# One-hot rows of the gate tables as products on VectorE, and the key lookup a tile at a time

## The chip, the cores and the metric

The kernel runs on one core of one Trainium2 chip. The metric is the device time of one execution in microseconds, as the median of several runs. Before the change it is 2661.93 us, the median of three runs (2655.82 to 2664.12).

## The reference, cut to what matters

One step of a decoder layer is computed for 512 prompt tokens and 8 x 4 sample tokens: retention, sparse attention with an indexer, two layer norms, and a layer of 128 x 128 = 16384 single-neuron experts. Only the experts' part touches the change:

```python
v1, i1 = lax.top_k(s1, PEER_TOPK)      # 16 best keys of 128, first half of the query
v2, i2 = lax.top_k(s2, PEER_TOPK)      # the same for the second half
cand = (v1[..., :, None] + v2[..., None, :]).reshape(T, PEER_HEADS, 256)
cidx = (i1[..., :, None] * PEER_NKEYS + i2[..., None, :]).reshape(T, PEER_HEADS, 256)
sc, sel = lax.top_k(cand, PEER_TOPK)   # 16 best sums of a head
eidx = jnp.take_along_axis(cidx, sel, axis=-1)
g = jax.nn.softmax(sc, axis=-1)
act = gelu(einsum('td,thkd->thk', xb, u[eidx]))
out = einsum('thk,thkd->td', g * act, v[eidx])
```

Each token has 8 heads, and each head chooses 16 experts, so a token has 128 triples of a first key, a second key and a gate.

## The kernel before, in words

The tokens stand in five tiles: four of 128 prompt tokens, and one with the sample group's 32 tokens four times over, on whose rows two heads stand where a prompt tile has eight. Matrix products in float32 are made of three products of two parts each (`mm3`); a weight's parts come from ScalarE (L126, the high part) and a subtract (L127, the low part, on VectorE or, for every other early product, on GpSimd).

Up to some 1320 us come the projections, the attention, the first layer norm and the scores of the keys. Then three stages follow.

*The choosing* (`choose`, L1187). For each tile VectorE finds the 16 best sums of each head, works out the place of each in the two lists, and looks up both keys. The lookup (L1243 to L1255) goes half by half and four heads at a time: GpSimd subtracts the numbers 0 to 15 (`iota`) from each place, so that a zero marks the place (L1247, `oh`, 128x1024); VectorE turns each head's zeros into the key there and everything else into 0 (L1251, 128x256, four of them); and VectorE adds each row of 16 (L1254). The tiles 0 and 4 come first, beside the embedding branch on TensorE; their experts are later fetched row by row. Then the three dense tiles 1, 2 and 3.

*The gate tables* (`gate_tables`, L1259). For a dense tile the chosen keys and gates are transposed by TensorE, so that the 128 choices stand on partitions and the tokens along the rows (`pkT`). For each token there are two one-hot matrices [128 choices, 128 keys]: `o1` for the first key, `o2` for the second, times the gate. Their product on TensorE (L1282) is the token's gates over all 128 x 128 experts. It goes eight tokens at a time: GpSimd subtracts the second key from the iota (L1273), VectorE compares the first key with the iota (L1275) and turns GpSimd's zeros into gates (L1277); all three are 128x1024. Four tokens' products fill a bank, ScalarE copies it out (L1283), and after 32 tokens a 2 MB store to DRAM follows. There are 3 tiles x 4 quarters of 32 tokens x 4 steps of eight, 48 steps. `o1` and `o2` have three buffers each.

*The experts* (from L1411). For 128 pieces of 128 experts TensorE makes the products with U (24 matmuls of 384 columns), gelu and gate follow, then the products with V (18 matmuls of 512 columns).

Two kinds of work fill waits: early products with U (`u_early`, L938), whose result goes to SBUF (22 of them at most, only while the tables are made) or to DRAM and back; and gathered rows (`gather_tile`, L1287): GpSimd issues an indirect DMA for one expert of each of 128 tokens (L1303), and VectorE uses it (L1316 for U, L1322 for V). A planner decides how many: each step of a stage yields the microseconds it claims of TensorE, VectorE and ScalarE, and `tick` (L953) adds them up and issues an early product (3.9 of TensorE) whenever the sum of TensorE is behind, and a row (1.15 of VectorE) for each 3.4 us of TensorE's sum. In `choose` the claims are `cost` = 0.85 (0.34 for the tile with two heads) times 0.8, four times 1.6, 3.0, 2.0 and, for the lookup, four times 2.3; the 48 steps of the tables claim 1.8, 2.3 and 1.2 each. Products that are not made early remain for the experts' stage.

Every engine works in the order of the code; loads are issued on SP's queue, stores on ScalarE's.

Of the kernel before, what the change touches and what calls it, by code (L numbers as in the profile page):

```python
# [11 lines left out]
F32 = mybir.dt.float32  # L12
F32R = mybir.dt.float32r
BF = mybir.dt.bfloat16
I32 = mybir.dt.int32
U32 = mybir.dt.uint32
AF = mybir.ActivationFunctionType
OP = mybir.AluOpType
AX = mybir.AxisListType
# [6 lines left out]
EPS = 1e-5  # L26
# [6 lines left out]
TOPK = 256  # L33
# [45 lines left out]
def tile_hybrid_step(ctx: ExitStack, tc: tile.TileContext, io):  # L79
# [24 lines left out]
    def moments(pieces, p0, p1, name):  # L104
        """1/sqrt(var + EPS) and -mean/sqrt(var + EPS) of the rows of [p, <= 512] views; the root by Newton's steps."""
# [23 lines left out]
    # ---------------------------------------------------------------- pools of the front  # L129
# [19 lines left out]
    def weights(src, n=1024, eng=V, raw=None, keep=None):  # L149
        """A [128, n] piece of a weight as its two float32r parts."""  # L150
        raw = raw or wst.tile([128, 1024], F32, name="wraw")
        load(raw[:, :n], src)
        h, l = keep or (wst.tile([128, 1024], F32R, name="wh"), wst.tile([128, 1024], F32R, name="wl"))
        split(h[:, :n], l[:, :n], raw[:, :n], eng)
        return h, l
# [21 lines left out]
    def project(chunk, evac):  # L177
        """Columns of a 128-wide chunk of W_in, transposed: [128, tokens]."""
# [8 lines left out]
    def project_nat(pieces, width, hook=lambda u: None, part=None):  # L187
        """Columns of W_in as they come: five tiles [128 tokens, columns]; pieces: (source, number of k), for width
        columns after the other. part: a tile for the sample group's four sums, each in 32 columns of the array (four
        k a piece); the fifth tile is then that group's alone."""  # L190
# [31 lines left out]
    def gates(n, tile_of):  # L222
        """Gates of the branches: the next chunks, as tanh(x / 2), to DRAM."""
# [6 lines left out]
    # ---------------------------------------------------------------- attention keys, indexer  # L230
# [29 lines left out]
    # places of the pages  # L260
# [17 lines left out]
    for i, t0 in enumerate(TILES):  # L278
# [3 lines left out]
        # keys of the attention, rotated  # L282
# [12 lines left out]
        # indexer keys: layer norm, rotated  # L295
# [43 lines left out]
    def rope_swap(dst, raw, cs, sn, blk, u, eng):  # L339
        """Rotation of rows in a chunk whose heads are blocks of 2*blk rows; sn has the source rows' signs."""  # L340
# [11 lines left out]
    # ---------------------------------------------------------------- queries of the attention  # L352
# [20 lines left out]
    # ---------------------------------------------------------------- indexer of the prompt  # L373
# [37 lines left out]
    # ---------------------------------------------------------------- indexer of the sample group  # L411
    # rows 32 q + 4 b + t: the q-th quarter of the past of token t of sequence b, then (q = 3) the new keys
# [64 lines left out]
    # the TOPK-th largest of each row, bit by bit; y = +-x so that it is not negative  # L477
# [6 lines left out]
    def row_sum(which):  # L484
        """Sum of cnt[:, which] over the four quarters of a row, on each of them."""
# [4 lines left out]
    def bisect_start():  # L490
        V.tensor_scalar(junk, scq, 0.0, None, op0=OP.is_ge, op1=OP.add, accum_out=cnt[:, 0:1])
        p = row_sum(0)
        # sign, and how many of y reach the value looked for
# [15 lines left out]
    def bisect_end():  # L509
# [3 lines left out]
        # how many of the equal ones are taken: the first of them  # L513
# [19 lines left out]
    # ---------------------------------------------------------------- retention  # L533
# [20 lines left out]
    def rotated(h, out):  # L554
        """q and k of a head, rotated; steps."""
# [15 lines left out]
    def group_norm(on, h, p, rows, sg, dst):  # L571
        """Rows of one head, normed over its 512 columns, turned, scaled and gated: dst [128, 4, rows]."""
# [11 lines left out]
    def head(h, prev, qk, ahead):  # L584
# [4 lines left out]
        # q, k  # L589
# [7 lines left out]
        # v  # L597
# [17 lines left out]
        # decayed k as it comes, for the states  # L615
# [9 lines left out]
        # sample: k four times over; parts of k and of the scores on rows 0:64 (high) and 64:128 (low)  # L625
# [20 lines left out]
        # gate  # L646
# [13 lines left out]
        def state_after():  # L660
            """State after the prompt."""
# [10 lines left out]
        # prompt: o[i] = sum over j <= i, two tiles of queries at a time  # L672
# [32 lines left out]
    def sample(h, kcs, srs, vst, qm, sgs):  # L705
        """Retention of the sample group, two sequences at a time."""
# [54 lines left out]
    # ---------------------------------------------------------------- queries, gates, attention of the prompt  # L761
    ASC = float(np.float32(128 ** -0.5))
    def softmax(x, src):
        """exp(ASC * (src - max)) / sum into x, over the rows of src."""
# [8 lines left out]
    def prompt_attention(aw):  # L773
        """The pieces of the attention of the prompt."""
# [32 lines left out]
    def sample_attention(st):  # L807
        """The pieces of the attention of the sample group, to be run one after another."""
# [18 lines left out]
        for g in range(2):  # L827
# [3 lines left out]
            for part in range(9):  # L831
# [13 lines left out]
            # of this part alone: its maximum, the sum of its exponentials, their product with V;  # L845
                # a part with no chosen key has zeros
# [22 lines left out]
            # the parts together  # L869
# [45 lines left out]
    # ---------------------------------------------------------------- rest of the layer up to PEER  # L915
# [5 lines left out]
    def layer_norm(x, rows, gb, eng=G):  # L921
        """In place, on a [rows, 1024] view."""
# [5 lines left out]
    # Work that fills the waits of the others: products with U whose V follows later, rows of the gathered experts.  # L928
# [24 lines left out]
    def tick(pe, dve, act=0.0):  # L953
        """After work of so many microseconds of the engines: as much of the filling as keeps them even."""
# [17 lines left out]
    def branch(rp, hook, done):  # L972
        """The sum of both branches, gated: its parts, [128, 8, tokens]. hook: other work, between the pieces; done:
        what has to come before the second branch, returns the pool of the result."""
# [46 lines left out]
    def project_out(hp, b4, brh, brl, brs):  # L1021
        """W_out and the residual: hs, [128 tokens, 1024] for each tile; steps for the tiles of FIRST."""
# [642 lines left out]
```

## Time and profile before

| | us |
|---|---|
| median of three runs | 2661.93 |
| profiled execution, span | 2726.3 |
| TensorE busy | 2478.5 |
| VectorE busy | 1934.1 |
| GpSimd busy | 993.5 |
| ScalarE busy | 953.4 |

The profiled execution gives its span, from the first to the last instruction; a time around it is not given. PE is TensorE, PEld its weight load, DVE VectorE, ACT ScalarE, POOL GpSimd, SP the queue of loads. A line of the table by stretches has the stretch and its length, then the busy time and the number of instructions of PE, PEld, DVE, ACT and POOL, the granted TensorE clock (1 is full), the DMA engines' busy share and GB/s. A line of the groups has source line, engine, operation, output and inputs, shapes and count, then the busy time in us and the mean ns of one, and at last the engine's idle time before them and what ended it. A line of the timeline has the start, the length, engine, line and operation; a bracket gives the idle time before it. An instruction's length includes the time that it was held up after its start.

### The profile page before, as it was taken

The page shows a single profiled execution, that of the slowest core. Times are in us where ns is not written, and L with a number is a line of the kernel's source. Part 1 is how long each engine was busy: PE and PEld are TensorE (multiplying, and loading weights), DVE is VectorE, ACT ScalarE, POOL GpSimd, SP SyncE. Part 2 cuts the span into 40 slices and gives each one's busy share as a digit, 9 for nine tenths or more (in the row PEclk, how much of TensorE's full clock was granted, in tenths as well). Part 3 has the DMA queues.
Part 4 walks back from the last instruction along what each step waited for, and adds up shares of the span by engine and source line. Part 5 has one row for each costly group of instructions (what it writes and reads, how often), then busy time and mean ns, then how long its engine had stood idle before and what let it go on. Part 6 is the DMA issues. An engine that isn't in the chain of part 4 may idle for free.

```text
span 2726.3 us, 40425 instructions
## 1 busy us (share of the span) xinstructions
PE 2478.5 (91%) x15162; PEld 2164.6 (79%) x15162; DVE 1934.1 (71%) x3867; ACT 953.4 (35%) x1657; POOL 993.5 (36%) x773
## 2 busy tenths in 40 slices
PE   8789999999988999999887777789999999999996
PEld 8768988888655569889777766778988988888885
DVE  6685667755322245578999999977777877877777
ACT  3232333333232333243222354543333333333332
POOL 4530000001134412110356778833444444443442
PEclk9889999999998999999998998899999999999998
DMA  6322243545675554232256566579888888998883
GB/s 204 106 85 92 71 167 113 195 127 191 226 227 156 152 173 160 96 138 72 93 184 203 201 224 223 206 259 349 294 317 310 315 321 306 332 319 308 300 314 126
DMA packets 233013, 562.71 MB, mean 206 GB/s; under 512 B 26576, under 2 KB 96400, under 8 KB 230896
## 3 DMA queue, kind: packets, MB, share of 16 engines
q1 hardware_dynamic: 140576, 287.83, 31.2%
q0 software_dynamic: 58368, 205.55, 21.6%
q10 hardware_dynamic: 33872, 66.73, 6.6%
q8 instruction: 119, 1.95, 0.3%
q14 instruction: 78, 0.64, 0.1%
HBM read 491.08 MB, written 68.95 MB: 205 GB/s over the span
## 4 chain that ended last, share of the span: by engine, by line
PE 65%; DVE 19%; issue 5%; DMA 4%; another core or an unknown queue 2%; ACT 2%; POOL 1%; SPq 0%; ACTq 0%; DVEq 0%; POOLq 0%
PE ps L160 7%; PE ps L158 7%; PE ps L159 7%; PE po L159 6%; PE po L158 6%; PE po L160 6%; PE act L158 4%; PE act L159 4%; PE act L160 4%; DVE o L1277 2%; DVE junk L1316 2%; PE nat L158 2%; PE nat L160 2%; DVE acc L1322 2%
## 5 line engine op out<-in xcount | busy, mean ns | idle before, releaser
L126 ACT ACTIVATE wh<-wraw 128x1024 fp32r<-128x1024 f32 (+2 forms) x265 | 278.7, 1052 | 606.3 <-PE ps L159 207.8
L127 DVE TENSOR_TENSOR wl<-wraw,wh 128x1024 fp32r<-128x1024 f32 (+2 forms) x239 | 306.0, 1280 | 172.7 <-ACT wh L126 150.1
L1303 POOL DMA_INDIRECT rows<-u_rows,eidx x160 | 240.3, 1502 | 317.8 <-DVE junk L1316 254.4
L1303 POOL DMA_INDIRECT rows<-v_rows,eidx x160 | 240.9, 1505 | 278.9 <-DVE acc L1322 192.5
L159 PE MATMUL po<-vl,ah 128*128 128x512 f32 x768 | 301.5, 393 | 6.6 <-DVE vl L127 6.6
L158 PE MATMUL po<-vh,ah 128*128 128x512 f32 x768 | 299.7, 392 | 1.1 <-ACT vh L126 1.1
L160 PE MATMUL po<-vh,al 128*128 128x512 f32 x768 | 300.1, 391 | 0.0
L158 PE MATMUL ps<-xh,wh 128*128 128x272 f32 x960 | 284.6, 296 | 9.3 <-issue 7.7
L159 PE MATMUL ps<-xl,wh 128*128 128x272 f32 x960 | 281.8, 294 | 8.1 <-issue 8.1
L160 PE MATMUL ps<-xh,wl 128*128 128x272 f32 x960 | 283.1, 295 | 5.9 <-issue 5.9
L160 PE MATMUL ps<-x1h,wl 128*128 128x384 f32 (+1 forms) x616 | 205.2, 333 | 28.4 <-DVE wl L127 16.8
L1322 DVE SCALAR_TENSOR_TENSOR acc<-rows,co,acc 128x1024 f32<-128x1024 f32 x160 | 227.1, 1420 | 4.4 <-DMA rows<-v_rows,eidx 3.8
L158 PE MATMUL act<-x1h,wh 128*128 128x384 f32 x664 | 225.2, 339 | 1.3 <-ACT gl L1456 1.3
L159 PE MATMUL act<-x1l,wh 128*128 128x384 f32 x664 | 223.3, 336 | 0.0
L160 PE MATMUL act<-x1h,wl 128*128 128x384 f32 x664 | 223.2, 336 | 0.0
L1316 DVE SCALAR_TENSOR_TENSOR junk<-rows,x1n 128x1024 bf16<-128x1024 f32 x160 | 212.7, 1329 | 5.8 <-DMA rows<-u_rows,eidx 5.3
L158 PE MATMUL ps<-x1h,wh 128*128 128x384 f32 (+1 forms) x616 | 206.4, 335 | 11.0 <-ACT pph L1179 8.0
L159 PE MATMUL ps<-x1l,wh 128*128 128x384 f32 (+1 forms) x616 | 202.7, 329 | 0.3 <-DVE x1l L1081 0.3
L158 PEld LDWEIGHTS ps<-xh,wh 128*128 128x128 f32 x960 | 185.6, 193 | 21.2 <-issue 13.9
L821 POOL DMA_INDIRECT kv<-ckv,idp x128 | 123.3, 963 | 211.2 <-PE nat L862 153.7
L159 PEld LDWEIGHTS ps<-xl,wh 128*128 128x128 f32 x960 | 185.8, 194 | 11.4 <-issue 10.6
L160 PEld LDWEIGHTS ps<-xh,wl 128*128 128x128 f32 x960 | 185.4, 193 | 8.1 <-issue 7.5
(448 smaller groups left out, 6121.5 us busy)
## 6 DMA issues: line engine op xcount, KB each, us to landing
wraw<-u_t SPq DMA_DIRECT2D x128, 512.0 KB
vr<-v_rows SPq DMA_DIRECT2D x128, 512.0 KB
wraw<-w_t SPq DMA_DIRECT2D x60, 512.0 KB
gg<-gd SPq DMA_DIRECT2D x33, 768.0 KB
gd<-stg ACTq DMA_DIRECT2D x12, 2048.0 KB
state<-state_ret SPq DMA_DIRECT2D x32, 512.0 KB
ret_sample<-state ACTq DMA_DIRECT2D x32, 512.0 KB
wraw<-w_rv SPq DMA_DIRECT2D x16, 512.0 KB
```

The source lines that it names most:

```text
L126: S.activation(h, x, AF.Copy)
L127: eng.tensor_tensor(l, x, r32(h), op=OP.subtract)
L158: T.matmul(out, lh, rh, start=first, stop=False)
L159: T.matmul(out, lh, rl, start=False, stop=False)
L160: T.matmul(out, ll, rh, start=False, stop=last)
L821: G.indirect_dma_start(out=kv[-1][:, i, :], out_offset=None, in_=io["ckv"], in_offset=bass.IndirectOffsetOnAxis(ap=idp[:, c:c + 1], axis=0))
L1277: V.scalar_tensor_tensor(o2, o2, 0.0, pkT[:, 2, tok, None].to_broadcast([128, 8, 128]), op0=OP.is_equal, op1=OP.mult)
L1303: G.indirect_dma_start(out=r, out_offset=None, in_=io[kind + "_rows"], in_offset=bass.IndirectOffsetOnAxis(ap=idx[:, p:p + 1], axis=0))
L1316: i = V.scalar_tensor_tensor(junk, r, 1.0, x, op0=OP.mult, op1=OP.mult, accum_out=dots[:, p % 16:p % 16 + 1])
L1322: i = V.scalar_tensor_tensor(acc, r, co[:, p % 16:p % 16 + 1], acc, op0=OP.mult, op1=OP.add)
```

## The change

Two places change. In the lookup both GpSimd's subtract and the division into groups of four heads go: for a whole tile and half, VectorE compares the places with the iota, multiplies by the keys, and adds the rows; the claims of these steps become 2.2 and 4.4 per half. In the tables each key is written as 8 a + b. For 32 tokens at a time VectorE makes one-hot rows of 16 for a and of 8 for b (with the gate in the second key's row of 8), and the one-hot row of 128 is their product, eight tokens an instruction. GpSimd has no part in either. The rest of the diff takes comments and docstrings out of the file.

```diff
@@ choose
-            for hh in range(0, nh, 4):
-                g = min(nh, 4)
-                oh = pw.tile([128, 16 * g, 16], F32, name="oh", tag="oh")
-                G.tensor_tensor(oh, abf[:, half, 16 * hh:16 * (hh + g), None].to_broadcast([128, 16 * g, 16]),
-                                iota[:, None, 0:16].to_broadcast([128, 16 * g, 16]), op=OP.subtract)
-                o4 = oh.rearrange("p (h k) a -> p h k a", h=g)
-                for h in range(g):
-                    V.scalar_tensor_tensor(o4[:, h], o4[:, h], 0.0,
-                                           ixf[:, hh + h, half, None, :].to_broadcast([128, 16, 16]),
-                                           op0=OP.is_equal, op1=OP.mult)
-                V.tensor_reduce(i12[:, half, 16 * hh:16 * (hh + g)], oh, AX.X, OP.add)
-                yield 0.0, cost * 2.3, 0.0
+            oh = pw.tile([128, n, 16], F32, name="oh", tag="oh")
+            V.tensor_tensor(oh, abf[:, half, :, None].to_broadcast([128, n, 16]),
+                            iota[:, None, 0:16].to_broadcast([128, n, 16]), op=OP.is_equal)
+            yield 0.0, cost * 2.2, 0.0
+            o4 = oh.rearrange("p (h k) a -> p h k a", h=nh)
+            V.tensor_tensor(o4, o4, ixf[:, :, half, None, :].to_broadcast([128, nh, 16, 16]), op=OP.mult)
+            V.tensor_reduce(i12[:, half, :], oh, AX.X, OP.add)
+            yield 0.0, cost * 4.4, 0.0
@@ gate_tables
+            up = gb.tile([128, 2, 128], I32, name="up", bufs=1)
+            lo = gb.tile([128, 2, 128], F32, name="lo", bufs=1)
+            upf = gb.tile([128, 2, 128], F32, name="upf", bufs=1)
+            V.tensor_copy(up, pkT[:, 0:2])
+            V.tensor_scalar(up, up, 3, None, op0=OP.logical_shift_right)
+            V.tensor_copy(upf, up)
+            V.scalar_tensor_tensor(lo, upf, -8.0, pkT[:, 0:2], op0=OP.mult, op1=OP.add)
             for q in range(4):
                 stg = gb.tile([128, 128, 32], F32, name="stg", bufs=2)
+                hot16 = gb.tile([128, 2, 32, 16], F32, name="hot16", bufs=1)
+                hot8 = gb.tile([128, 2, 32, 8], F32, name="hot8", bufs=1)
+                tq = slice(32 * q, 32 * q + 32)
+                for half in range(2):
+                    V.tensor_tensor(hot16[:, half], upf[:, half, tq, None].to_broadcast([128, 32, 16]),
+                                    iota[:, None, 0:16].to_broadcast([128, 32, 16]), op=OP.is_equal)
+                    V.tensor_tensor(hot8[:, half], lo[:, half, tq, None].to_broadcast([128, 32, 8]),
+                                    iota[:, None, 0:8].to_broadcast([128, 32, 8]), op=OP.is_equal)
+                V.tensor_tensor(hot8[:, 1], hot8[:, 1], pkT[:, 2, tq, None].to_broadcast([128, 32, 8]), op=OP.mult)
                 for c in range(0, 32, 8):
-                    tok = slice(32 * q + c, 32 * q + c + 8)
+                    ct = slice(c, c + 8)
                     o1 = gb.tile([128, 8, 128], F32, name="o1", bufs=3)
                     o2 = gb.tile([128, 8, 128], F32, name="o2", bufs=3)
-                    G.tensor_tensor(o2, iota[:, None, :].to_broadcast([128, 8, 128]),
-                                    pkT[:, 1, tok, None].to_broadcast([128, 8, 128]), op=OP.subtract)
-                    V.tensor_tensor(o1, iota[:, None, :].to_broadcast([128, 8, 128]),
-                                    pkT[:, 0, tok, None].to_broadcast([128, 8, 128]), op=OP.is_equal)
-                    V.scalar_tensor_tensor(o2, o2, 0.0, pkT[:, 2, tok, None].to_broadcast([128, 8, 128]),
-                                           op0=OP.is_equal, op1=OP.mult)
+                    for half, o in enumerate((o1, o2)):
+                        V.tensor_tensor(o.rearrange("p t (a b) -> p t a b", b=8),
+                                        hot16[:, half, ct, :, None].to_broadcast([128, 8, 16, 8]),
+                                        hot8[:, half, ct, None, :].to_broadcast([128, 8, 16, 8]), op=OP.mult)
```

## Rows read from the trace of the kernel before

**Rows 1.** The page's busy line: engine, us, share of the span, instructions.
```profile
PE 2478.5 (91%) x15162; PEld 2164.6 (79%) x15162; DVE 1934.1 (71%) x3867; ACT 953.4 (35%) x1657; POOL 993.5 (36%) x773
```
**Rows 2.** Busy time by stretches: the choosing, the tables, the experts.
```profile
1320.00:1525.00 205.00, 162.36 (x965) 151.17 (x965) 198.17 (x522) 55.49 (x102) 115.22 (x62) 0.91 0.54 178
1525.00:1812.00 287.00, 211.42 (x1288) 200.17 (x1288) 279.47 (x183) 137.67 (x165) 224.76 (x107) 0.89 0.61 214
1812.00:2726.00 914.00, 884.60 (x4306) 784.07 (x4304) 689.05 (x919) 325.19 (x464) 370.48 (x250) 0.99 0.84 301
```
**Rows 3.** Chain of waits by line: first the tables' stretch, then the experts'.
```profile
by line: DVE o L1277 20.6%; issue 18.6%; DVE junk L1316 15.7%; DVE o L1275 14.0%; DVE acc L1322 13.7%; DVE wl L127 6.2%; DMA rows<-v_rows,eidx 2.0%; POOL o L1273 1.9%; PE nat L1282 1.2%; POOL rows L1303 1.2%; POOL wl L127 1.2%; PE ps L159 0
...
by line: PE po L159 17.3%; PE po L158 17.2%; PE po L160 17.1%; PE act L158 11.4%; PE act L159 11.3%; PE act L160 11.3%; DMA gl<-act_d 3.1%; DMA gg<-gd 1.4%; issue 1.4%; DVE vl L127 1.2%; DVE acc L1322 1.0%; DMA rows<-u_rows,eidx 0.9%; DVE l
```
**Rows 4.** Groups of instructions in the tables' stretch, 1525 to 1812 us.
```profile
L1282 PE MATMUL nat<-o,o 128*128 128x128 f32 x768 | 116.2, 315 | 68.2 <-DVE o L1277 65.0 <-DVE co L1321 2.1 <-ACT stg L1283 1.1
L1273 POOL TENSOR_TENSOR o<-iota,pkT 128x1024 f32<-128x1024 f32 x48 | 112.1, 2339 | 12.5 <-PE nat L1282 9.3 <-ACT pkT L1266 2.5
...
L1275 DVE TENSOR_TENSOR o<-iota,pkT 128x1024 f32<-128x1024 f32 x48 | 89.3, 1860 | 0.0
L1277 DVE SCALAR_TENSOR_TENSOR o<-o,pkT 128x1024 f32<-128x1024 f32 x48 | 80.0, 1666 | 0.0
...
L1316 DVE SCALAR_TENSOR_TENSOR junk<-rows,x1n 128x1024 bf16<-128x1024 f32 x26 | 49.5, 1903 | 0.0
L1322 DVE SCALAR_TENSOR_TENSOR acc<-rows,co,acc 128x1024 f32<-128x1024 f32 x22 | 48.7, 2212 | 0.0
...
L127 POOL TENSOR_TENSOR wl<-wraw,wh 128x1024 fp32r<-128x1024 f32 x10 | 30.1, 3014 | 1.8 <-ACT wh L126 1.8
```
**Rows 5.** VectorE's timeline at two places of the tables' stretch.
```profile
1610.55 1.22 DVE L1275 TENSOR_TENSOR o<-iota,pkT 128x1024 f32<-128x1024 f32 x1
1611.69 1.21 DVE L1277 SCALAR_TENSOR_TENSOR o<-o,pkT 128x1024 f32<-128x1024 f32 x1
...
1632.61 2.91 DVE L1275 TENSOR_TENSOR o<-iota,pkT 128x1024 f32<-128x1024 f32 x1
1635.44 2.91 DVE L1277 SCALAR_TENSOR_TENSOR o<-o,pkT 128x1024 f32<-128x1024 f32 x1
```
**Rows 6.** GpSimd's timeline: a fetch beside idle VectorE, subtracts, a fetch beside busy VectorE.
```profile
1524.25 0.93 POOL L1303 DMA_INDIRECT rows<-v_rows,eidx  x1 [0.66 <-DVE acc L1322]
...
1632.40 2.04 POOL L1273 TENSOR_TENSOR o<-iota,pkT 128x1024 f32<-128x1024 f32 x1
1634.94 2.34 POOL L1273 TENSOR_TENSOR o<-iota,pkT 128x1024 f32<-128x1024 f32 x1 [0.50 <-PE nat L1282]
...
1803.94 1.68 POOL L1303 DMA_INDIRECT rows<-u_rows,eidx  x1 [2.86 <-DVE junk L1316]
```
**Rows 7.** VectorE's timeline in the choosing: 256, 512 and 192 columns.
```profile
1335.30 0.41 DVE L1251 SCALAR_TENSOR_TENSOR oh<-oh,ixf 128x256 f32<-128x256 f32 x1
...
1337.97 0.67 DVE L127 TENSOR_TENSOR wl<-wraw,wh 128x512 fp32r<-128x512 f32 x1
...
1409.92 0.34 DVE L1201 TENSOR_TENSOR cand<-tv 128x192 f32<-128x192 f32 x1
```
**Rows 8.** Groups of instructions in the choosing's stretch, 1320 to 1525 us.
```profile
L1251 DVE SCALAR_TENSOR_TENSOR oh<-oh,ixf 128x256 f32<-128x256 f32 x68 | 43.1, 670 | 3.7 <-POOL oh L1247 3.7
...
L1247 POOL TENSOR_TENSOR oh<-abf,iota 128x1024 f32<-128x1024 f32 (+1 forms) x18 | 36.7, 2048 | 39.6 <-ACT tg L1178 16.7 <-DVE pick L1254 7.6 <-DVE abf L1225 7.6
```
**Rows 9.** ScalarE's groups before the experts: results of early products, to DRAM and kept.
```profile
L947 ACT ACTIVATE early<-ps 128x384 f32<-128x384 f32 x25 | 11.9, 475 | 2.6 <-PE ps L160 2.1 <-DVE tg L1180 0.5
L944 ACT ACTIVATE kept<-ps 128x384 f32<-128x384 f32 x20 | 9.7, 487 | 15.0 <-PE ps L160 15.0
```
**Rows 10.** TensorE's groups in the experts' stretch: a third of the products with U.
```profile
L158 PE MATMUL act<-x1h,wh 128*128 128x384 f32 x662 | 224.5, 339 | 1.3 <-ACT gl L1456 1.3
```

## The prediction

> **What bounds the kernel now.** I read the page first: TensorE is busy 91% of the span, VectorE 71%, GpSimd 36% [rows 1]. An average over such different stages says little, so the next view was the table by stretches [rows 2]. Its three lines are the three stages that this change can reach: the choosing of experts (1320 to 1525 us), the gate tables (1525 to 1812) and the experts (1812 to the end). VectorE is busy 198.2 of 205 us in the first and 279.5 of 287 in the second, TensorE only 162 and 211; in the third TensorE has 884.6 of 914 and VectorE 689. The chain of waits, taken stretch by stretch, agrees [rows 3]: in the tables five lines of VectorE work lead it, and the experts' chain is almost all matmul. So VectorE sets the end of the tables, TensorE that of the experts.
>
> Next, what VectorE does for 287 us. The groups of the tables' stretch [rows 4] have 48 pairs of L1275 and L1277 and 48 gathered rows (26 of L1316, 22 of L1322), all 128x1024 but with means from 1666 to 2212 ns. The timeline tells why [rows 5]: the same instruction takes 1.21 us at one place and 2.91 at another. Undelayed, two of them start 1.14 us apart (1610.55, 1611.69); delayed, 2.83 (1632.61, 1635.44). What differs is GpSimd: its subtract L1273 begins at 1632.40, just before the long one [rows 6]. A GpSimd elementwise instruction thus holds up VectorE for 2.83 - 1.14 = 1.7 us. The excess over 1.21 us in four groups of rows 4 (31 + 22 + 18 + 22 us) is 93 us; with VectorE's splits it comes near 58 x 1.7 = 99, for 48 subtracts and the 10 splits that GpSimd does. Much of VectorE's busy time in the tables is waiting.
>
> **The tables, part by part.**
> Taken away: 48 subtracts of GpSimd, 48 x 1.70 = -81.6 us of VectorE's time. Their bounds: 0 if other work of GpSimd moves into the place, and 48 x 2.04 = -98 if an instruction is held for the whole length of theirs. I take 1.70, which stands in the rows.
> [...]
> Replaced: 96 one-hot instructions of 128x1024 by 96 products of that size. No row has such a product. The nearest is L1201's addition of 128x192, whose first operand repeats an element eight times and whose second repeats a run of eight, as in the product: it takes 0.34 us [rows 7]. With 0.41 us for 256 columns and 0.67 for 512, 192 would be 0.34 on the same line, so repetition costs nothing there. Zero, with bounds from 0 to +96 x 1.07 (a second pass over 1024 columns, 2 x (1.21 - 0.67), at each product).
> Added: for each of 12 quarters two instructions of 128x512 and three of 128x256. An instruction's place in a full queue is 0.07 us shorter than its length (1.21 and 1.14 above), so 2 x 0.60 + 3 x 0.34 = 2.22, by 12 = +26.6. For each of three tiles four small ones on 256 columns, 4 x 0.34 x 3 = +4.1. They could be dearer only by a GpSimd split that falls on them, which it does to any instruction.
> Together -50.9.
>
> **The filling.** The planner's credits change too, since the lookup's steps now claim 2 x 6.6 = 13.2 units per tile instead of 4 x 2.3 = 9.2. A dense tile credits VectorE 0.85 x 25.4 = 21.6 instead of 18.2 us; three tiles 10.2 more. Each 3.4 us of TensorE credit brings a gathered row, which credits VectorE 1.15, so 10.2 / (1 - 1.15 / 3.4) = 15.4 us must be filled: 4 more early products with U at 3.9, and 5 more rows. Running the credits through step by step gives 25 + 20 = 45 early products before, as the trace has them [rows 9], and 28 + 21 after; three of the four fall in the choosing, one in the tables, and of the rows three and two. Each early product takes its 512 KB load on SP's queue and its split with it; the kept one stays in SBUF, the other three add a store on ScalarE's queue and a load. During the first tiles' choosing TensorE's credit is ahead either way, so nothing is added. Cost in the tables: one early product (its split alternates between VectorE, 1.14, and GpSimd, about 2.1 of holding up: 1.6) and two rows at 1.21, +4.0. Tables in all: **-46.9 us**, 287 to about 240. What is late next there is TensorE, with 211 us busy and about 4 more.
>
> **The choosing.** An 8-head tile loses 4 subtracts of GpSimd and, on VectorE, 16 x 0.34 + 4 x 1.14 = 10.0; it gains six instructions of 2048 columns at 2.22 (1.14 plus twice the 0.54 that lies between 512 and 1024 columns) = 13.3, so +3.3. The tile with two heads goes from 4 x 0.34 + 2 x 0.60 = 2.6 to 6 x 0.60 = 3.6, +1.0. Holding up: L1251 alone shows (0.670 - 0.411) x 68 = 17.6 us, the floor for 18 subtracts [rows 8]; the ceiling is 18 x 1.7 = 30.6. I take 1.4 each, near the middle, because other instructions are hit too. First tiles (six subtracts, two of half size): -7 + 3.3 + 1.0 = **-2.7**. Dense tiles (twelve): -16.8 + 9.9, then three early products and three rows, 3 x 1.6 + 3 x 1.21 = 8.4: **+1.5**.
>
> **The experts.** Four products with U have left a stretch that TensorE bounds. On the chain they have 11.4 + 11.3 + 11.3 = 34% of 914 us for 662 / 8 = 83 of them [rows 3, 10], 3.75 each: -15.0. Three of the four come back from DRAM; such loads have 3.1% of that chain for 25 of them, 1.13 each: +3.4. Both together **-11.6**; bounds -17 and 0, the latter if memory and not TensorE bounds this stretch.
>
> Sum: -46.9 - 2.7 + 1.5 - 11.6 = -59.7 of 2726.3 us of profiled span (what lies around it is not shown). The median of the runs, 2661.9, is 0.976 of that, so -58: **2603 us**.
>
> **Rivals.**
> *TensorE or ScalarE takes the place.* In the tables TensorE waited 65 us for L1277 [rows 4]; a shorter VectorE may leave it waiting for its own order (an early product stands between two tokens' groups). Against: 215 us fit in 240, and three buffers of each one-hot tile decouple them. If half the tables' gain goes so, -36 x 0.976: 2627.
> *Fetches are starved.* GpSimd's row fetch takes 0.93 us when VectorE idles and 1.68 when it works [rows 6]. With no subtracts between, VectorE works without pause. If every fourth of 50 rows then came 5 us late, 60 us go and the time is 2661. Against: at 1803.94 VectorE also worked without pause, and the fetch still took 1.68.
> *Slower: the repeated operand streams slowly.* The place is the 96 products, each reading one element eight times running. The price is up to 1.07 us each, +103, hence 2603 + 0.976 x 103 = 2703; it decides from 59.7 / 96 = 0.62 us a product on. For it: a run of eight over 1024 columns is in no row. Against it: L1201 [rows 7], and L1275, which reads one element 128 times running at the full 1.21 [rows 5].
> [...]
>
> **How the numbers follow.** The forecast has 0.75, TensorE in its place 0.13, starved fetches 0.05, the slow operand 0.07. Within 0.3% (8 us, about what a measurement of this kernel can tell from none) counts the starved case: faster 0.88, same 0.05, slower 0.07. The range goes from 2583 (the holding up at its ceiling everywhere) to 2645 (half of the tables' gain and all of the experts' lost, with some 7 us more).
>
> **What would show it.** Right: L1273 and L1247 gone; the products near 1.21 us with a spread only where GpSimd splits; the stage of the tables about 240 us with VectorE still above 90%; 49 early products (28 + 21), 79 products with U in the experts, which take some 12 us less. Wrong: products at 1.9 us or above; waits of VectorE for rows; idle time of TensorE in the tables that VectorE didn't cause; an experts' stretch as long as before.

## The result, and the profile after

The changed kernel takes 2599.06 us (median of four runs, 2597.81 to 2602.69), the kernel before 2660.26 (four runs); the ratio is 0.9768, with a 95% interval of 0.9755 to 0.9782. The forecast was 2603, with a range of 2583 to 2645.

The page's busy line of the changed kernel (its profiled execution took 2597.81 us, of which the span is 2596.0):

```profile
PE 2435.0 (94%) x15162; PEld 2126.6 (82%) x15162; DVE 1871.1 (72%) x3881; ACT 950.4 (37%) x1661; POOL 884.8 (34%) x709
```

The two spans differ by 130 us, the medians by 61. So I cut both traces at the same instructions: from the first L1201 to the tables' first transposes (choosing), to the last copy `stg` (tables), to the end (experts). First the kernel before, cut so, then the changed kernel; columns as in [rows 2], the first line being what lies ahead of the choosing.

```profile
0.00:1312.40 1312.40, 1212.55 (x8547) 1022.73 (x8548) 759.78 (x2182) 432.72 (x925) 283.00 (x355) 0.96 0.44 144
1312.40:1528.90 216.50, 173.86 (x1049) 161.54 (x1049) 205.77 (x584) 58.99 (x107) 117.80 (x63) 0.91 0.54 181
1528.90:1811.50 282.60, 207.02 (x1263) 195.81 (x1262) 279.47 (x183) 135.99 (x162) 222.17 (x105) 0.89 0.60 212
1811.50:2726.30 914.80, 885.10 (x4309) 784.57 (x4307) 689.05 (x919) 325.69 (x465) 370.48 (x250) 0.99 0.84 301
```

```profile
0.00:1248.10 1248.10, 1195.37 (x8547) 1010.33 (x8548) 759.41 (x2182) 431.46 (x925) 291.31 (x355) 0.98 0.47 151
1248.10:1461.90 213.80, 180.26 (x1121) 166.53 (x1121) 202.21 (x535) 63.66 (x112) 100.17 (x49) 0.96 0.61 198
1461.90:1694.90 233.00, 191.87 (x1287) 182.44 (x1286) 231.02 (x261) 134.57 (x166) 118.17 (x61) 0.96 0.74 261
1694.90:2596.00 901.10, 867.47 (x4213) 767.34 (x4211) 678.42 (x906) 320.68 (x460) 375.17 (x246) 0.99 0.84 302
```

Ahead of the choosing the same instructions run in both (PE 8547, DVE 2182), yet one execution took 1312.4 us there and the other 1248.1. That is 64 of the 130 us, and it isn't the change's: among the experiments below, for this same code, the three profiles from the chip on which the kernel before takes 2662 us have 1245 to 1250 us there, and those from chips on which it takes 2740 to 2746 us have 1302 to 1342. The rest is what the change can reach: choosing -2.7, tables -49.6, experts -13.7, together -66.0. The reader sees VectorE still busy in the tables for 231.0 of 233.0 us, but with 48 us less to do.

The groups of the tables' stretch, after (columns as in [rows 4]):

```profile
L1287 DVE TENSOR_TENSOR o<-hot,hot 128x1024 f32<-128x1024 f32 x96 | 119.8, 1281 | 0.0
L1293 PE MATMUL nat<-o,o 128*128 128x128 f32 x768 | 99.2, 286 | 25.8 <-DVE o L1287 23.0 <-ACT stg L1294 1.1 <-ACT kept L944 0.9
...
L1314 POOL DMA_INDIRECT rows<-u_rows,eidx x32 | 47.2, 1475 | 81.1 <-DVE junk L1327 55.3 <-PE nat L1293 13.8 <-DVE acc L1333 8.9
L1314 POOL DMA_INDIRECT rows<-v_rows,eidx x19 | 44.6, 2346 | 31.5 <-DVE acc L1333 15.5 <-PE nat L1293 7.9 <-DVE junk L1327 5.2
L1327 DVE SCALAR_TENSOR_TENSOR junk<-rows,x1n 128x1024 bf16<-128x1024 f32 x31 | 39.8, 1283 | 0.0
...
L1333 DVE SCALAR_TENSOR_TENSOR acc<-rows,co,acc 128x1024 f32<-128x1024 f32 x18 | 27.2, 1513 | 0.7 <-DMA rows<-v_rows,eidx 0.7
L127 POOL TENSOR_TENSOR wl<-wraw,wh 128x1024 fp32r<-128x1024 f32 x10 | 27.2, 2721 | 2.6 <-ACT wh L126 2.4
...
L1277 DVE TENSOR_TENSOR hot<-upf,iota 128x512 f32<-128x512 f32 x24 | 19.2, 801 | 0.0
...
L1279 DVE TENSOR_TENSOR hot<-lo,iota 128x256 f32<-128x256 f32 x24 | 12.5, 519 | 0.0
```

The chain of waits through this stretch, by line (against the first line of [rows 3]):

```profile
by line: DVE o L1287 30.5%; issue 22.1%; DVE junk L1327 13.8%; DVE acc L1333 6.3%; DMA rows<-v_rows,eidx 5.8%; DVE hot L1279 4.6%; DVE wl L127 3.6%; DVE hot L1277 3.3%; PE nat L1293 1.8%; DVE hot L1281 1.7%; DMA act_d<-early 1.6%; DVE up L1
```

It is still led by VectorE's lines. Against [rows 4]: 96 one-hot instructions went from 89.3 + 80.0 us to 119.8, and 48 or 49 gathered rows from 98.2 to 67.0, though nothing in the change touches the code of the rows. The wait of TensorE for VectorE's one-hot tiles went from 65.0 to 23.0 us.

VectorE's timeline in the tables, after: products in an open stretch, and a gathered row that GpSimd's split holds up.

```profile
1502.82 0.41 DVE L1279 TENSOR_TENSOR hot<-lo,iota 128x256 f32<-128x256 f32 x1
1503.15 1.21 DVE L1287 TENSOR_TENSOR o<-hot,hot 128x1024 f32<-128x1024 f32 x1
1504.29 0.41 DVE L1281 TENSOR_TENSOR hot<-hot,pkT 128x256 f32<-128x256 f32 x1
...
1510.31 3.41 DVE L1327 SCALAR_TENSOR_TENSOR junk<-rows,x1n 128x1024 bf16<-128x1024 f32 x1
```

```profile
1510.09 2.55 POOL L127 TENSOR_TENSOR wl<-wraw,wh 128x1024 fp32r<-128x1024 f32 x1
```

The product, with an element repeated eight times, takes the 1.21 us of the undelayed 128x1024 instructions before [rows 5]. The early products, after (against [rows 9]):

```profile
L947 ACT ACTIVATE early<-ps 128x384 f32<-128x384 f32 x28 | 13.3, 475 | 0.5 <-PE ps L160 0.4
L944 ACT ACTIVATE kept<-ps 128x384 f32<-128x384 f32 x21 | 10.3, 491 | 17.9 <-PE ps L160 17.9
```

### The profile page after: what moved, and what is told of

The parts are those of the page before. It is cut to its first block, busy times and chain, and to the rows that moved or that the text cites. A ratio compares the mean times of both kernels' runs of the same rounds, so it can differ in the third digit from the quotient of the medians.

```text
span 2596.0 us, 40358 instructions
## 1 busy us (share of the span) xinstructions
PE 2435.0 (94%) x15162; PEld 2126.6 (82%) x15162; DVE 1871.1 (72%) x3881; ACT 950.4 (37%) x1661; POOL 884.8 (34%) x709
## 4 chain that ended last, share of the span: by engine, by line
PE 65%; DVE 17%; DMA 6%; issue 6%; POOL 4%; ACT 2%; SPq 0%; ACTq 0%; DVEq 0%; POOLq 0%
PE ps L158 6%; PE ps L160 6%; PE ps L159 6%; PE po L159 6%; PE po L158 6%; PE po L160 6%; PE act L158 4%; PE act L159 4%; PE act L160 4%; DVE o L1287 3%; PE nat L158 3%; PE nat L841 2%; PE nat L160 2%; PE nat L159 2%; POOL kxs L452 2%
## 5 line engine op out<-in xcount | busy, mean ns | idle before, releaser
L127 DVE TENSOR_TENSOR wl<-wraw,wh 128x1024 fp32r<-128x1024 f32 (+2 forms) x237 | 290.9, 1228 | 136.2 <-ACT wh L126 130.6
L1314 POOL DMA_INDIRECT rows<-v_rows,eidx x160 | 264.1, 1650 | 343.2 <-DVE acc L1333 189.2
L160 PE MATMUL ps<-x1h,wl 128*128 128x384 f32 (+1 forms) x648 | 212.3, 329 | 32.8 <-POOL wl L127 17.5
L158 PE MATMUL act<-x1h,wh 128*128 128x384 f32 x632 | 215.2, 341 | 5.8 <-ACT gl L1467 5.8
L1333 DVE SCALAR_TENSOR_TENSOR acc<-rows,co,acc 128x1024 f32<-128x1024 f32 x160 | 217.3, 1358 | 1.5 <-DMA rows<-v_rows,eidx 0.9
L158 PE MATMUL ps<-x1h,wh 128*128 128x384 f32 (+1 forms) x648 | 212.5, 328 | 5.3 <-ACT pph L1179 3.6
L159 PE MATMUL act<-x1l,wh 128*128 128x384 f32 x632 | 213.2, 337 | 0.0
L160 PE MATMUL act<-x1h,wl 128*128 128x384 f32 x632 | 213.2, 337 | 0.0
L159 PE MATMUL ps<-x1l,wh 128*128 128x384 f32 (+1 forms) x648 | 209.3, 323 | 0.3 <-DVE x1l L1081 0.3
L1327 DVE SCALAR_TENSOR_TENSOR junk<-rows,x1n 128x1024 bf16<-128x1024 f32 x160 | 198.3, 1239 | 8.4 <-DMA rows<-u_rows,eidx 8.1
L160 PEld LDWEIGHTS ps<-xh,wl 128*128 128x128 f32 x960 | 182.0, 190 | 5.4 <-DVE wl L127 4.8
```

What stands on the lines that cost most here:

```text
L127: eng.tensor_tensor(l, x, r32(h), op=OP.subtract)
L158: T.matmul(out, lh, rh, start=first, stop=False)
L159: T.matmul(out, lh, rl, start=False, stop=False)
L160: T.matmul(out, ll, rh, start=False, stop=last)
L1314: G.indirect_dma_start(out=r, out_offset=None, in_=io[kind + "_rows"], in_offset=bass.IndirectOffsetOnAxis(ap=idx[:, p:p + 1], axis=0))
L1327: i = V.scalar_tensor_tensor(junk, r, 1.0, x, op0=OP.mult, op1=OP.mult, accum_out=dots[:, p % 16:p % 16 + 1])
```

## The experiments

All are edits of the changed kernel. Stage lengths come from each run's own profile, cut as above. The ratio is to the kernel before, run beside each on the same chip. Early products ahead of the experts: to DRAM + kept.

| run | choosing | tables | experts | early | ratio, 95% interval |
|---|---|---|---|---|---|
| before | 216.5 | 282.6 | 914.8 | 25+20 | 1 |
| changed kernel | 213.8 | 233.0 | 901.1 | 28+21 | 0.9768, 0.9755 to 0.9782 |
| changed kernel, again | 216.6 | 232.8 | 902.7 | 28+21 | 0.9782, 0.9707 to 0.9856 |
| tables alone | 214.2 | 231.9 | 912.1 | 25+20 | 0.9791, 0.9735 to 0.9847 |
| lookup alone | 213.4 | 287.8 | 905.9 | 28+21 | 0.9974, 0.9937 to 1.001 |
| subtract put back | 214.3 | 321.6 | 901.2 | 28+21 | 1.0053, 1.0006 to 1.01 |
| write only | 214.1 | 234.2 | 903.5 | 28+21 | 0.9745, 0.9677 to 0.9812 |
| plain compare | 213.4 | 260.1 | 904.5 | 28+21 | 0.9844, 0.9753 to 0.9936 |
| old claims | 193.6 | 235.9 | 912.6 | 25+20 | 0.9726, 0.964 to 0.9812 |
| splits on VectorE | 194.4 | 231.4 | 900.5 | 28+21 | 0.9672, 0.9583 to 0.9762 |
| fewer rows | 202.8 | 218.3 | 923.6 | 28+21 | 0.9734, 0.9706 to 0.9761 |
| fewer rows, splits on VectorE | 181.0 | 198.3 | 925.8 | 28+21 | 0.9644, 0.9616 to 0.9673 |
| old claims, splits on VectorE | 187.6 | 228.9 | 914.4 | 25+20 | 0.9713, 0.9682 to 0.9744 |
| lookup's subtracts put back | 215.4 | 237.9 | 919.6 | 25+20 | 0.981, 0.9737 to 0.9883 |

**The halves.** The lookup's lines as before the change, then the tables' lines as before.

```diff
@@ tables alone: choose
-            V.tensor_tensor(oh, abf[:, half, :, None].to_broadcast([128, n, 16]),
-                            iota[:, None, 0:16].to_broadcast([128, n, 16]), op=OP.is_equal)
...
+                G.tensor_tensor(oh, abf[:, half, 16 * hh:16 * (hh + g), None].to_broadcast([128, 16 * g, 16]),
+                                iota[:, None, 0:16].to_broadcast([128, 16 * g, 16]), op=OP.subtract)
...
```

> The gate tables as in the changed kernel, the lookup and its claims as before. Theory (GpSimd's 48 subtracts held up VectorE by 1.70 us each; the new small instructions cost 30.7 us; nothing else moves): -81.6 + 30.7 = -51 us against the kernel before, about 2610 us, with 45 early products as before and the tables' stretch near 230 us. Rival (the gain comes from the early products that the new claims move out of the experts' stage): no gain here, about 2650 us or more.

> The lookup a tile at a time with its new claims, the gate tables as before. Theory: by the prediction's terms -2.7 and +1.5 in the choosing, +4 in the tables for one more early product and two rows, -11.6 in the experts' stage: -9 us, about 2651 us. Rival (the moved products make the gain): most of the 61 us, about 2605 us.

The tables alone take 50.7 us from their own stage and next to nothing from the others; the lookup alone takes 3.1 from the choosing and 8.9 from the experts, and adds 5.2 to the tables (forecast for the added early product and rows there: +4.0). The sums by stages, -55.7 and -6.8, add up to -62.5 against -66.0 for the whole, and the two ratios multiply to 0.9765 against 0.9768: the two edits are additive.

**The subtract.** Both put a GpSimd instruction of 128x1024 ahead of each pair of products, its result unread; the one reads SBUF, the other only writes.

```diff
+                    g0 = gb.tile([128, 8, 128], F32, name="g0", bufs=1)
+                    tok = slice(32 * q + c, 32 * q + c + 8)
+                    G.tensor_tensor(g0, iota[:, None, :].to_broadcast([128, 8, 128]),
+                                    pkT[:, 1, tok, None].to_broadcast([128, 8, 128]), op=OP.subtract)
@@ write only: this line instead
+                    G.memset(g0, 0.0)
```

> The changed kernel, and in each of the 48 steps GpSimd again subtracts the second key from the iota, 128x1024, into a tile that nobody reads. Theory (an elementwise instruction of GpSimd that reads SBUF holds up VectorE's two-input instructions by about 1.70 us): +75 to +82 us, about 2677 us, with products and gathered rows of up to 2.9 us in the tables. Rival (the subtracts ran beside VectorE, and what went was the wait for their result): within 5 us of 2599.

> The changed kernel, and in each of the 48 steps GpSimd writes zeros to a 128x1024 tile that nobody reads; it reads nothing. [...] Rival (any elementwise instruction of GpSimd holds up VectorE for most of its length): 48 times 0.8 to 1.7 us more, 2640 to 2680 us.

The tables' stretch with the subtract put back, and its groups:

```profile
1547.00:1868.60 321.60, 208.23 (x1288) 198.99 (x1286) 307.81 (x261) 135.32 (x166) 224.90 (x109) 0.81 0.54 189
```

```profile
L1291 DVE TENSOR_TENSOR o<-hot,hot 128x1024 f32<-128x1024 f32 x96 | 140.7, 1498 | 6.4 <-PE nat L1297 6.4
L1288 POOL TENSOR_TENSOR g<-iota,pkT 128x1024 f32<-128x1024 f32 x48 | 116.5, 2428 | 5.7 <-ACT pkT L1262 3.1
...
L1337 DVE SCALAR_TENSOR_TENSOR acc<-rows,co,acc 128x1024 f32<-128x1024 f32 x18 | 36.6, 2036 | 6.2 <-DMA rows<-v_rows,eidx 6.1
```

The write-only one:

```profile
L1289 DVE TENSOR_TENSOR o<-hot,hot 128x1024 f32<-128x1024 f32 x96 | 120.0, 1283 | 0.0
...
L1287 POOL MEMSET g<- 128x1024 f32 x48 | 46.0, 959 | 1.8
```

An instruction that nobody reads makes the tables 88.8 us longer than in the changed kernel's second run (232.8; 75 to 82 were expected), 1.85 each. Of these, 307.81 - 230.15 = 77.7 us are added to VectorE's busy time, 1.62 each; the rest is waiting, such as the 6.1 us for rows and 6.4 for TensorE that the groups show. The memset, 48 times 0.96 us on the same engine, costs 1.4 us in all, where the rival had 48 times 0.8 to 1.7, and the products beside it take 1283 ns in the mean, as they do without it (1281 ns in the changed kernel), against 1498 beside the subtract. So here GpSimd's being busy and its writing did not hold VectorE up; what the subtract has beyond the memset is the reading of two inputs from SBUF. The two also differ in length and operation, and no instruction that reads one input was tried.

**Plain compare.** No factors: per step of eight tokens VectorE compares both keys with the iota and multiplies by the gate, three instructions of 128x1024 for two.

```diff
...
+                    for half, o in enumerate((o1, o2)):
+                        V.tensor_tensor(o, iota[:, None, :].to_broadcast([128, 8, 128]),
+                                        pkT[:, half, tok, None].to_broadcast([128, 8, 128]), op=OP.is_equal)
+                    V.tensor_tensor(o2, o2, pkT[:, 2, tok, None].to_broadcast([128, 8, 128]), op=OP.mult)
```

> The changed kernel, with the one-hot rows of the tables made without factors: VectorE compares both keys with the iota (two instructions of 128x1024 a step) and multiplies the second by the gate (a third one), GpSimd has no part. Theory (VectorE's work sets the tables' stretch): 48 x 1.14 = 54.7 us more of VectorE and 30.7 less, +24 us against the changed kernel; against the kernel before still -37 us. Rival (once GpSimd is gone another engine sets the stretch): within 5 us of the changed kernel.

The tables are 27.3 us longer. Three instructions at 1.14 for 48 steps are 164 us, and two with the 30.7 us of small ones 140: 24 us by the prediction's own prices. So VectorE still sets this stage, and the factors are worth 27.3 us; GpSimd's subtract, put back above, costs 88.8.

**Old claims.** The new lookup, but its steps claim 2 x 2.3 per half tile as the old ones did, so that the filling stays as before.

```diff
-            yield 0.0, cost * 2.2, 0.0
+            yield 0.0, cost * 2.3, 0.0
...
-            yield 0.0, cost * 4.4, 0.0
+            yield 0.0, cost * 2.3, 0.0
```

> The changed kernel, but the lookup's steps claim 2.3 and 2.3 per half and not 2.2 and 4.4, so that the planner's sums are those of the kernel before (45 early products). Theory (the prediction's terms: the filling costs 8.4 us in the choosing and 4 in the tables and gives 11.6 back in the experts' stage): the same time as the changed kernel within 3 us, the choosing 8 and the tables 4 us shorter, the experts' stage 12 longer. Rival (early products go into time that TensorE has to spare and cost nothing): 10 to 13 us more than the changed kernel.

Without the added filling the choosing takes 193.6 us. The lookup itself is thus worth 20.6 (against the tables alone, 214.2), and the added filling costs 20 to 23 there (213.8 and 216.6). For these two the prediction had -9.6 and +8.4. The tables, expected 4 us shorter, are 3 longer (235.9), and by the sum of its stages this run is 10 us shorter than the changed kernel's second run, which neither its theory nor its rival had; the intervals of the two ratios overlap. The copies of early products on ScalarE show their pace at the end of the choosing, after:

```profile
1421.21 0.47 ACT L947 ACTIVATE early<-ps 128x384 f32<-128x384 f32 x1
1426.62 0.47 ACT L947 ACTIVATE early<-ps 128x384 f32<-128x384 f32 x1
...
1458.37 0.48 ACT L947 ACTIVATE early<-ps 128x384 f32<-128x384 f32 x1
```

There are seven in 37.2 us, one every 6.2, where such a product takes 3.75 on the experts' chain [rows 3, 10]: their splits stand in turn in VectorE's queue, behind lookup instructions of 2.28 us and gathered rows, and in GpSimd's, behind fetches. The tables' first transposes stand behind them on TensorE. VectorE's own time grows as much: with the filling it is busy for 204.6 us of the choosing (second run) against 182.0 with the old claims, 22.7 more, with 31 rows for 25.

**Where the splits stand.** All splits of early products on VectorE, with the new claims and with the old.

```diff
-        p = u_dots(*weights(io["u_t"][j], eng=G if j % UPOOL else V))
+        p = u_dots(*weights(io["u_t"][j], eng=V))
```

> The changed kernel, with every early product's split on VectorE, where GpSimd did every other one; the planner's sums are unchanged. Theory (a split of GpSimd's holds VectorE up by about 2 us, one on VectorE takes 1.14): 24 splits, about 0.9 us each, -15 to -20 us, most of it -9 in the tables and -10 in the choosing. Rival (GpSimd's splits fall into VectorE's idle time): +24 x 1.14 = +27 us.

> The changed kernel with the lookup's claims as before (25 + 20 early products) and all splits of the early products on VectorE. Theory (the four early products added cost more in the choosing than they give back among the experts, wherever their splits stand): about 10 us shorter than with the splits alone, choosing about 182 us, experts about 912, ratio about 0.963. Rival (it was the splits' place, in turn behind GpSimd's fetches and VectorE's lookup, that made the filling dear, and with all of them on VectorE four more products cost what they give back): no shorter than with the splits alone, ratio 0.967 to 0.971, choosing about 185 to 190.

With the new claims the choosing falls by 22.2 us against the second run of the changed kernel (the theory had 10 there and 9 in the tables), and the experts keep what the four early products give. With the old claims on top it falls only 7 more, the experts lose 14, and the ratio is no lower: the filling is no loss once all its splits stand on VectorE. The theory of that second run (the filling costs more than it returns, wherever the splits stand) fell, its rival holds. But two things go with GpSimd's splits, their turn behind the fetches and their holding up of VectorE: it makes 27 splits in the choosing for 16, and yet its busy time falls from 204.6 to 180.8 us. These runs do not tell the two apart. In the tables the splits gave 1.4 us only. GpSimd's fetches there, with splits on VectorE:

```profile
L1314 POOL DMA_INDIRECT rows<-u_rows,eidx x32 | 72.0, 2252 | 68.6 <-DVE junk L1327 61.0 <-DVE up L1267 2.8 <-issue 1.8
L1314 POOL DMA_INDIRECT rows<-v_rows,eidx x21 | 64.8, 3087 | 38.4 <-DVE acc L1333 21.2 <-DVE junk L1327 13.5 <-DVE up L1267 2.9
```

In the mean a fetch is some 0.75 us longer than after the change alone (1475 and 2346 ns).

**The lookup's subtracts put back**, on top of the old claims, at their old places and unread.

```diff
+            for hh in range(0, nh, 4):
+                g = min(nh, 4)
+                g0 = pw.tile([128, 64, 16], F32, name="g0", bufs=1)
+                G.tensor_tensor(g0[:, :16 * g], abf[:, half, 16 * hh:16 * (hh + g), None].to_broadcast([128, 16 * g, 16]),
+                                iota[:, None, 0:16].to_broadcast([128, 16 * g, 16]), op=OP.subtract)
```

> The changed kernel with the lookup's claims as before (choosing 194, tables 236, experts 913 us in its own run), and in it the 18 subtracts of the old lookup put back on GpSimd at their old places (16 of 128x1024, 2 of 128x512), their results unread. It tells how much of the choosing's time they held. Theory (in the choosing they hold VectorE as long as they do in the tables, 1.85 us for 128x1024, since whatever stands next on VectorE is held): 17 x 1.85 = 31 us, choosing about 225 us, longer than the 214 to 216 of the old lookup because the new lookup's own instructions are some 10 us longer; the rest unchanged; ratio about 0.984. Rival (the prediction's size, 1.4 us each, since short instructions and gaps take a part of the holding): +25 us at most, choosing 215 to 219. Second rival (TensorE or GpSimd's own order set part of the choosing, so that the subtracts cost less than 1 us each): choosing under 212.

The choosing with them, and without (the run with old claims):

```profile
1309.90:1525.30 215.40, 167.84 (x1026) 155.15 (x1026) 209.07 (x525) 58.03 (x105) 123.46 (x60) 0.90 0.52 173
```

```profile
1329.80:1523.40 193.60, 165.58 (x1027) 154.76 (x1026) 181.95 (x527) 58.51 (x105) 89.81 (x43) 0.92 0.59 195
```

+21.8 us, 1.28 for each 128x1024 (16 and two halves are 17): my theory of 1.85 fell, and the prediction's size, 1.4, is the nearer. VectorE's busy time rises by 27.1, 1.60 each, as in the tables; but here VectorE sat idle for 11.7 us, and 5.3 of that took up a part.

The tables alone have the same subtracts and the old lookup's short instructions on VectorE, and take 214.2 us in the choosing. So the longer instructions of the new lookup cost 1.2 us in place of the short ones, where the prediction adds 14.2.

**Fewer rows.** The planner's credits are set so that 28 + 21 early products remain, but it issues 15 rows in the choosing and 25 in the tables, for 29 and 50; then the same with the splits on VectorE.

```diff
-CF = 0.85
+CF = 1.053
...
-RATE = 1 / 3.4
-GY = (1.8, 2.3, 1.2)
+RATE = 1 / 6.8
+GY = (1.8, 2.9, 1.2)
```

> The changed kernel with its filling set sparser, so that it still makes 28 + 21 early products ahead of the experts but reads 15 rows in the choosing and 25 in the tables (29 and 50 in the changed kernel); the 39 rows left over are read among the experts. Theory (VectorE still sets choosing and tables; among the experts it has room: 678 of 903 us busy): a row costs VectorE 1.32 us (66 us for 50 in the repeated run of the changed kernel), so the tables lose 25 x 1.32 = 33 us (TensorE's 194 us busy is the floor, so to about 200), the choosing 14 x 1.3 = 18 us, the experts grow by little: about -45 us, ratio about 0.962. Rival (the experts are bound by what the DMA moves, 302 GB/s): the 39 rows of 0.5 MB are 20 MB more there, +66 us, so about +15 us, ratio about 0.983. A second rival: what is freed on VectorE in the tables is taken by the wait for ScalarE or TensorE, tables no shorter than 220 us.

> The kernel with the sparser rows and, beside that, all splits of the early products on VectorE instead of every second one on GpSimd. Theory: the two are additive: splits on VectorE took 19 to 22 us from the choosing and 1 us from the tables, so about -65 us against the changed kernel, ratio about 0.955. Rival (experts bound by the DMA): experts longer by 66 us, and the total about equal to the changed kernel's.

The stages of the second one:

```profile
1249.80:1430.80 181.00, 171.23 (x1120) 161.35 (x1119) 175.93 (x533) 62.30 (x111) 38.98 (x23) 1.00 0.60 196
1430.80:1629.10 198.30, 181.97 (x1289) 177.30 (x1288) 192.30 (x223) 132.39 (x164) 120.38 (x25) 0.99 0.65 240
1629.10:2554.90 925.80, 878.37 (x4212) 771.55 (x4210) 722.49 (x968) 318.88 (x461) 435.57 (x284) 0.98 0.88 316
```

Fewer rows alone give -11.0, -14.7 and +22.5 us, -3.2 together, where the theory had -45: the rows among the experts are not free (0.6 us each), though far from the rival's 66, and the ratio, 0.9734, lies between theory (0.962) and rival (0.983). The second rival (tables no shorter than 220) nearly holds with 218.3, and falls once the splits move. With the splits on VectorE as well, the choosing and the tables come near what TensorE needs (171 of 181, 182 of 198), and the time is **2563.21 us**, ratio 0.9644 (the theory had 0.955): faster than both kernels (2662.33 for the one before, beside it; 2599.06 after the change). The chain of waits of its tables shows what is next, the rows' own arrival with 16.3%, and their fetches:

```profile
by line: DVE o L1287 31.2%; DMA rows<-v_rows,eidx 16.3%; issue 9.6%; DVE wl L127 8.2%; PE nat L1293 6.5%; DVE acc L1333 5.4%; POOL rows L1314 4.9%; DVE hot L1279 3.0%; DVE hot L1277 3.0%; PE ps L158 2.0%; PE ps L159 2.0%; PE ps L160 2.0%; D
```

```profile
L1314 POOL DMA_INDIRECT rows<-v_rows,eidx x13 | 78.8, 6059 | 30.4 <-DVE acc L1333 25.9 <-DVE lo L1270 2.1 <-issue 0.9
```

## Why the prediction was right, step by step

| step | forecast | measured |
|---|---|---|
| tables | -46.9 | -49.6 |
| choosing | -2.7 + 1.5 | -2.7 |
| experts | -11.6 | -13.7 |
| sum | -59.7 | -66.0 by stages, -61.2 by the medians |

**The bound.** That VectorE sets the tables and that much of its busy time was holding up is shown by the subtract put back (88.8 us), and from the other side by the plain compare (27.3).

**The tables.** 1.70 us a subtract lies between the 1.62 that each adds to VectorE's busy time and the 1.85 that it adds to the stage. The products cost nothing more than what they replace (1.21 us, and 96 of them 119.8 with what splits still hold up). The 30.7 us for the small instructions are confirmed through the plain compare, 27.3 for 24. The rival of TensorE in VectorE's place didn't come: TensorE's wait for VectorE's tiles is still 23.0 us of the stage, and VectorE idles for 2.0. VectorE's held instructions stood to the end of GpSimd's: the two held instructions of [rows 5] end 1.07 to 1.08 us after the subtracts of [rows 6] (1635.52 after 1634.44, 1638.35 after 1637.28), the gathered row at 1510.31 above ends 1.08 us after the split at 1510.09, and in the trace of the kernel before all 48 subtracts show 1.08. So VectorE stood still to that end each time and then needed its own time. The price is nevertheless 1.70 (2.91 less 1.21) and not the subtract's 2.04, the prediction's bound for an instruction held for the whole length: VectorE's held instruction began 0.21 us after the subtract at 1632.40. With VectorE idle a subtract takes 1.90 us:

```profile
1759.93 1.90 POOL L1288 TENSOR_TENSOR g<-iota,pkT 128x1024 f32<-128x1024 f32 x1
```

This line is from the run with the subtract put back. The price in the sum was right, though VectorE was held to the subtract's end.

**The choosing** came out near its -1.2 by luck: two terms of the sum were wrong, and their errors cancel. The holding up was sized well, 1.28 measured for 1.4. The first wrong term is the longer instructions on VectorE, "+3.3" for a tile and "+1.0", together 14.2: they cost 1.2 (215.4 with the subtracts put back, 214.2 in the tables alone), so the lookup gave 20.6 us and not 9.6. Of the 13 us between, the old lookup's wait for the subtracts' results accounts for at most 3.6 (L1251's group in the tables alone; 3.7 in [rows 8]), since an unread subtract is not waited for; what the rest is stays open. The second is "three early products and three rows, 3 x 1.6 + 3 x 1.21", 8.4: the filling cost 20 to 23 us. With all splits on VectorE it costs 6.8, so it is the splits on GpSimd that the term had wrong; whether by their turn in the queues or by their holding up of VectorE is not separated.

**The experts.** On the full set of rows, six other runs with 28 + 21 early products have 900.5 to 905.9 us there, and four with 25 + 20 have 912.1 to 919.6; with the two main profiles the means are 902.8 and 914.7. So -11.9 for -11.6; the -13.7 of the one pair has the spread of single profiles in it.

**The scale.** I scaled the sum by 0.976, the median over the profile's span, as if the excess of that execution were spread over all of it. It lies ahead of the choosing (1312.4 for 1248.1; the changed kernel's three stages differ by 2.8 us at most between its two runs), so the sum should have stood unscaled: 1.4 us.

**The other rivals.** Starved fetches: not here. VectorE waits 0.7 us for rows in the groups; but the chain of the tables now has 5.8% for rows in flight (2.0% before, [rows 3]), and in the fastest version it is 16.3%, where the rival has come (see the last section). The slow operand is excluded by 1.21 us.

## What to carry to other kernels

A busy share near 100% on VectorE is not yet work: compare the length of one instruction beside a reading GpSimd instruction and beside none (here 2.91 and 1.21 us), and price the GpSimd instruction by that (1.70), not by its own length (2.04). Once it is gone, the next gain is in the filler work that was fitted to the old stage: here moving half the splits and thinning the gathered rows gave 36 us beyond the change's 61. Price a filler by what its instructions do on every engine they stand on: here it cost the choosing 20 to 23 us with half of the splits on GpSimd, and 6.8 with all of them on VectorE.

## What had not been expected of the hardware

A row fetch on GpSimd was held up for as long as VectorE worked without a pause, 27.86 us. Beside an idle VectorE one took 0.93 us [rows 6]. The mean (U and V rows) is 1475 and 2346 ns after the change, 2252 and 3087 with the splits on VectorE too, 3480 and 6059 in the fastest version's tables, of which these are lines:

```profile
1507.62 27.86 POOL L1314 DMA_INDIRECT rows<-v_rows,eidx  x1 [0.66 <-DVE acc L1333]
1535.78 0.94 POOL L1314 DMA_INDIRECT rows<-v_rows,eidx  x1 [0.30 <-issue]
```

```profile
1533.41 1.25 DVE L127 TENSOR_TENSOR wl<-wraw,wh 128x1024 fp32r<-128x1024 f32 x1
1540.00 1.28 DVE L1333 SCALAR_TENSOR_TENSOR acc<-rows,co,acc 128x1024 f32<-128x1024 f32 x1 [5.33 <-DMA rows<-v_rows,eidx]
```

From the start of the long fetch to 1534.66 VectorE's instructions follow each other without a gap; the fetch ends 0.82 us after the last of them, and then VectorE waits 5.33 us for the row. It is not VectorE's busy share that decides (97% there, 99% after the change). Other fetches beside a busy VectorE take 1.68 us (at 1803.94 before the change [rows 6], at 1615.04 after it); what lets those through is not shown.

The 768 matmuls of the tables took 99.2 us for 116.2, with the granted clock at 0.96 of full on average for 0.89, while TensorE was busy 82% of the stage for 73%; with the subtract put back it was busy 65% and the clock 0.81.
